# The DeltaNet's per-partition products as scaled copies on ScalarE, in a two-layer decoder trunk

## The chip, the cores and the metric

The kernel runs on one core of one Trainium2 chip. The metric is device time in microseconds for one launch of the whole trunk: 512 tokens of width 1024 through two layers. Weights and activations are fp32; TensorE's products are made of three passes on split operands (a high part `hi` rounded to fp32r, and the low part `x - hi`), so every weight that is loaded is first split by ScalarE (the high part) and VectorE (the low part).

## The reference

Each layer is a half-step SwiGLU, a mixer, a second half-step SwiGLU and a gated per-layer embedding, with an RMSNorm ahead of each. The mixer makes one input projection and parts its columns among an RG-LRU, sliding-window attention and a gated DeltaNet. Only the last is touched by the change. Per head (4 heads of width 64) and per chunk of 64 tokens it computes:

```python
gcum = jnp.cumsum(gc, axis=-1)
decay = jnp.exp(jnp.where(tril, gcum[..., :, None] - gcum[..., None, :], -jnp.inf))
k_beta = kc * bc[..., None]
v_beta = vc * bc[..., None]
Lmat = jnp.where(strict, jnp.einsum('...id,...jd->...ij', k_beta, kc) * decay, 0.0)
T = lax.linalg.triangular_solve(Lmat + eye, jnp.broadcast_to(eye, Lmat.shape), left_side=True,
                                lower=True, unit_diagonal=True)
u = jnp.einsum('...ij,...jd->...id', T, v_beta)
w = jnp.einsum('...ij,...jd->...id', T, k_beta * jnp.exp(gcum)[..., None])
```

and then a scan over chunks: `v_new = u - w @ state`, an output, and `state = state * exp(g_last) + k_dec^T @ v_new` with `k_dec = k * exp(g_last - g)`.

## The kernel before

Tokens lie on partitions in four tiles of 128 (`t` = 0 to 3); a tile holds two chunks of 64, and each tile carries the four heads side by side. The function `mixer` (called once per layer) issues, in this order: the projections that DeltaNet needs (`proj(0)` to `proj(5)`, and the product `ptm` in token layout), the small vectors (`beta`, `g`, norms), and then the DeltaNet stages below. Between them the call `fill(next(gaps, 0))` issues pieces of the rest of the mixer (the remaining projections `pp`, attention, RG-LRU), so that TensorE has work while the DeltaNet chain goes on; `GAPS` says how many microseconds of such pieces stand in each gap, and `ORDER` in which order they come.

TensorE's order is that of the program (`manual_schedule` for PE). The other engines' instructions are put in order by a scheduler that takes, from the instructions that are ready in its own timeline, the earliest in the program; those inside `tc.high_priority()` (the splits of `weight`, L119 on ScalarE and L120 on VectorE) come first. On the chip each engine then works through its queue strictly in that order.

The stages that the change touches:

- `masked(t)` (L1207 to L1213): for the high and the low part of `g`, the triangle `tri` (128x128) times one number per partition and head, into a tile `tg` of 128x512. One GpSimd instruction for each part. TensorE sums the two over partitions into `R` (L1220), the decay's exponent.
- `chunk(t)` (L1215 to L1257): `R`, the products `pk` of keys and queries with keys (L1227), the decay `DT` from `R` on ScalarE (L1231, L1233), its mask and scale on VectorE (L1236), the entries of `LTA` and `aT` (L1246, L1248), `er` and `qg`, and last `vk[t]`'s upper half (the keys times `eg`, L1252) and `kd[t]` (the keys times `cd`, L1255), each one GpSimd instruction of 128x256.
- the calls, in program order: `masked(0)`, `masked(1)`, a gap, the small products `pc` with `gc`, `eg`, `cd` and `egl`, and then for each `t`: `chunk(t)`, a gap, `masked(t + 2)`.
- `pv`: the values are transposed by TensorE, two tiles at a time, and VectorE scales them by `vr` into `vk[t]`'s lower half (L1289).
- Behind these, VectorE inverts the triangular blocks: transposes L1300, fifteen steps of substitution (L1310 to L1312), `TMA` (L1317), and TensorE joins the blocks in two levels (`pinv`, L1332, L1339, L1344), where ScalarE copies `pn` (L130). `vk` is first used by `products(0)` (L1381), `kd` by `steps(0)` (L1402).

The tiles `tg`, `DT`, `vk` and several others come from one pool of 14 slots (tag `d`). In the same stretch `fill` issues `lru_conv`: ScalarE's first tap (L875) and VectorE's three others (L877).

Of the kernel before, what the change touches and what calls it, by code (L numbers as in the profile page):

```python
# [9 lines left out]
F32 = mybir.dt.float32  # L10
# [4 lines left out]
AF = mybir.ActivationFunctionType  # L15
ALU = mybir.AluOpType
# [42 lines left out]
def trunk(ctx: ExitStack, tc: tile.TileContext, a):  # L59
    nc = tc.nc  # L60
    V, A, G, T = nc.vector, nc.scalar, nc.gpsimd, nc.tensor
# [7 lines left out]
    def bank(shape, name):  # L69
        return banks.tile(shape, F32, tag="b", name=name)  # L70
# [11 lines left out]
    tri = cst[:, K_TRI:K_TRI + 128]  # L82
# [742 lines left out]
    def mixer(l, norm, gain, ahead):  # L825
        xh, xl = norm.xh, norm.xl
        pl = par[:, l, :]
        with ExitStack() as es:
# [7 lines left out]
            def d2(shape, name):  # L836
                return dp.tile(shape, F32, tag="d", name=name)
# [17 lines left out]
            def small(name, n=16, **kw):  # L855
                return tp.tile([128, n], F32, tag=name, name=name, **kw)
# [209 lines left out]
            def fill(us):  # L1066
                while us > 0:
                    c = next(fill_, None)
                    if c is None:
                        return  # L1070
                    us -= c
# [28 lines left out]
            ktm = Pair([2, 128], "ktm")  # L1100
# [18 lines left out]
            for p in range(2):  # L1119
                pt = bank([128, 2, 2, 128], "ptk")  # L1120
                for i in range(2):
                    t = 2 * p + i
# [11 lines left out]
            def v3(x):  # L1134
# [7 lines left out]
                            in1=pl[:, C_DTB:C_DTB + 4].unsqueeze(1).to_broadcast([128, NT, 4]), op=ALU.add)  # L1142
# [5 lines left out]
            def hc(x):  # L1148
# [8 lines left out]
                                   in1=ea.unsqueeze(1).to_broadcast([128, NT, 4]),  # L1157
# [7 lines left out]
            vr = small("vr")  # L1165
# [36 lines left out]
            vk = [d2([128, 4, 128], "vk") for t in range(NT)]  # L1202
            aT = [None] * NT
            kd = Pair([2, 128], "kd")
# [3 lines left out]
            def masked(t):  # L1208
                tg[t] = [dp.tile([128, 4, 128], F32R, tag="d", name="tg") for x in range(2)]
                for o, x in zip(tg[t], (gh, gl_)):  # L1210
                    G.tensor_tensor(out=o, in0=tri.unsqueeze(1).to_broadcast([128, 4, 128]),
                                    in1=x.bitcast(F32)[:, 4 * t:4 * t + 4].unsqueeze(2).to_broadcast([128, 4, 128]),
                                    op=ALU.mult)  # L1213

            def chunk(t):  # L1215
                tsl = slice(t * 128, (t + 1) * 128)

                R = bank([128, 4, 128], name="R")
                for i, x in enumerate(tg[t]):
                    T.matmul(out=R.rearrange("p h i -> p (h i)"), lhsT=ones_r, rhs=x.rearrange("p h i -> p (h i)"),  # L1220
                             start=i == 0, stop=i == 1)

                pks = [bank([128, 2, 2, 128], "pk") for hh in range(2)]
                for c in range(2):
                    for hh in range(2):
                        r0 = 64 * hh
                        T.matmul(out=pks[hh][:, c], lhsT=kq[r0:r0 + 64, c, 0, tsl], rhs=kq[r0:r0 + 64, c, :, tsl],  # L1227
                                 start=True, stop=True)
                DT = d2([128, 4, 128], "DT")
                for h in range(4):  # L1230
                    A.activation(out=DT[:, h, :], in_=R[:, h, :], func=AF.Relu, scale=-1.0,  # L1231
                                 bias=gc[:, 4 * t + h:4 * t + h + 1])
                A.activation(out=DT, in_=DT, func=AF.Exp, scale=-1.0)  # L1233

                for h in range(4):
                    V.scalar_tensor_tensor(out=DT[:, h, :], in0=DT[:, h, :], scalar=b2[:, 4 * t + h:4 * t + h + 1],  # L1236
                                           in1=tri, op0=ALU.mult, op1=ALU.mult)
                er = small("er", 256)
                for hh in range(2):
                    rs = slice(64 * hh, 64 * hh + 64)  # L1240
                    A.activation(out=er[rs].rearrange("p (c i) -> p c i", c=2), in_=R[rs, 2 * hh:2 * hh + 2, :],
                                 func=AF.Exp)
                G.tensor_tensor(out=qg[t], in0=kq[:, :, 1, tsl], in1=er.rearrange("p (c i) -> p c i", c=2),
                                op=ALU.mult)
                for hh, pk in enumerate(pks):
                    V.tensor_tensor(out=LT[t][:, 2 * hh:2 * hh + 2, :], in0=pk[:, :, 0, :],  # L1246
                                    in1=DT[:, 2 * hh:2 * hh + 2, :], op=ALU.mult)
                    V.tensor_tensor(out=DT[:, 2 * hh:2 * hh + 2, :], in0=pk[:, :, 1, :],  # L1248
                                    in1=DT[:, 2 * hh:2 * hh + 2, :], op=ALU.mult)
                aT[t] = DT  # L1250
                kv = ktm[t].rearrange("p c (h d) -> p h c d", h=2)
                G.tensor_tensor(out=vk[t][:, :, 64:128].rearrange("p (h c) d -> p h c d", h=2), in0=kv,  # L1252
                                in1=eg[:, 4 * t:4 * t + 4].rearrange("p (h c) -> p h c", h=2).unsqueeze(3)
                                .to_broadcast([128, 2, 2, 64]), op=ALU.mult)
                G.tensor_tensor(out=kd[t].rearrange("p c (h d) -> p h c d", h=2), in0=kv,  # L1255
                                in1=cd[:, 4 * t:4 * t + 4].rearrange("p (h c) -> p h c", h=2).unsqueeze(3)
                                .to_broadcast([128, 2, 2, 64]), op=ALU.mult)  # L1257

            fill(next(gaps, 0))
            masked(0)  # L1260
            masked(1)
            fill(next(gaps, 0))
            pc = bank([128, 4, 16], "pc")
# [4 lines left out]
            eg = small("eg")  # L1268
            A.activation(out=eg, in_=pc[:, 0, :], func=AF.Exp)
            cd = small("cd")  # L1270
# [5 lines left out]
            for t in range(NT):  # L1276
                chunk(t)
                fill(next(gaps, 0))
                if t + 2 < NT:
                    masked(t + 2)  # L1280
            for p in range(2):
                pv = bank([128, 2, 2, 128], "pv")
                for i in range(4):
                    t = 2 * p + i // 2
                    T.transpose(out=pv[:, i // 2, i % 2, :], in_=s2[i % 2][:, t * 128:(t + 1) * 128], identity=ident)
                for i in range(2):
                    t = 2 * p + i

                    V.tensor_tensor(out=vk[t][:, :, 0:64].rearrange("p (h c) e -> p h c e", h=2),  # L1289
                                    in0=pv[:, i].rearrange("p c (h e) -> p h c e", h=2),  # L1290
                                    in1=vr[:, 4 * t:4 * t + 4].rearrange("p (h c) -> p h c", h=2).unsqueeze(3)
                                    .to_broadcast([128, 2, 2, 64]), op=ALU.mult)
                fill(next(gaps, 0))


# [2 lines left out]
            for q in range(4):  # L1298
                rs = slice(32 * q, 32 * q + 32)
                V.transpose(out=l32[rs].rearrange("p u j -> p (u j)"),  # L1300
                            in_=LTA[rs].rearrange("p t h i -> p (t h) i")[:, :, 32 * q:32 * q + 32])
# [11 lines left out]
            for t in range(NT):  # L1313
                if t == 0:
# [3 lines left out]
                                in0=x16[:, 4 * t:4 * t + 4, :].unsqueeze(2).to_broadcast([128, 4, 8, 16]),  # L1318
                                in1=cst[:, K_B16:K_B16 + 8].unsqueeze(1).unsqueeze(3).to_broadcast([128, 4, 8, 16]),
                                op=ALU.mult)  # L1320
# [170 lines left out]
            o = PAIRED  # L1491
# [7 lines left out]
            for c in range(2):  # L1499
                py = bank([128, S], "py")  # L1500
                for t in range(NT):
                    T.transpose(out=py[:, t * 128:(t + 1) * 128],
                                in_=oo[t // 2][:, t % 2, 2 * c:2 * c + 2, :].rearrange("p h e -> p (h e)"), identity=ident)
# [122 lines left out]
    for l in range(L):  # L1626
        pl = par[:, l, :]
        norm = rest(f, norm, pl[:, C_MX:C_MX + 8])
        f = ffn(l, 2)
        norm = mixer(l, norm, pl[:, C_F2:C_F2 + 8], f)  # L1630
        norm = rest(f, norm, pl[:, C_PL:C_PL + 8])
        f = ffn(l + 1, 1) if l + 1 < L else None
        norm = ple(l, norm, par[:, l + 1, C_F1:C_F1 + 8] if f else None, f)
# [123 lines left out]
```

## Time and profile before

| what | value |
| --- | --- |
| median of 3 runs (lowest to highest) | 2029.34 us (2026.89 to 2031.62) |
| the profiled execution's own time | 2028.79 us |
| its span | 2027.0 us |
| TensorE busy | 1975.1 us (97% of the span) |
| VectorE busy | 1485.6 us (73%) |
| ScalarE busy | 988.1 us (49%) |
| GpSimd busy | 142.7 us (7%) |
| chain that ended last: TensorE | 86% of the span |

TensorE is PE in the rows, ScalarE ACT, VectorE DVE, GpSimd POOL. A timeline row has the start and the duration in us from the span's start, the engine, the line, the operation, the tiles (out<-in), the shape and the count; where several were merged, the duration covers all of them. Square brackets hold the idle time of the engine just before and what ended it. Neighbouring instructions of one engine overlap a little, so starts are the safer measure of pace. PEclk is TensorE's granted clock as a share of full speed.

### The profile page before, as it was taken

Reading aid. Unit: us, or ns where it says so; the run is one execution under the profiler, and the core shown is the slowest. Engines: PE = TensorE matmul, PEld = TensorE weight load, DVE = VectorE, ACT = ScalarE, POOL = GpSimd, SP = SyncE. Lnnn points to the kernel's source line nnn. Section 1 sums busy time; section 2 is a strip of 40 time slices with the busy share of each in tenths; the row PEclk is TensorE's granted clock in tenths of the full one; section 3 lists DMA queues with packets and bytes.
Section 4 is the critical chain, followed back from the end, with each engine's and each line's share of the span. In section 5 each row is a group of like instructions: output and inputs, shape, how many; then the busy total and the mean of one; then the engine's idle time right before and its main releaser. Section 6 shows DMA issues by size and latency. Waiting matters only on the chain.

```text
span 2027.0 us, 32034 instructions
## 1 busy us (share of the span) xinstructions
PE 1975.1 (97%) x12657; PEld 1757.5 (87%) x12657; DVE 1485.6 (73%) x2603; ACT 988.1 (49%) x1633; POOL 142.7 (7%) x170
## 2 busy tenths in 40 slices
PE   8999999998999999999999999999899999999997
PEld 7988998886779989998889799988676899899886
DVE  6875873889868856865788568657887787488466
ACT  5643552455745534543555346434375555255343
POOL 0000000041200000000000000000311000000000
PEclk8999999998999999999999999999999999999998
DMA  6753743221053735745337357423112367275421
GB/s 212 190 168 100 187 119 121 79 73 55 9 166 101 203 112 147 179 124 135 120 101 201 105 150 176 124 80 104 53 34 68 105 172 183 78 193 138 134 66 63
DMA packets 83687, 249.79 MB, mean 123 GB/s; under 512 B 9424, under 2 KB 16848, under 8 KB 83280
## 3 DMA queue, kind: packets, MB, share of 16 engines
q1 hardware_dynamic: 72016, 205.79, 31.8%
q0 software_dynamic: 11520, 41.95, 11.8%
q8 instruction: 99, 1.62, 0.3%
q14 instruction: 52, 0.43, 0.1%
HBM read 245.61 MB, written 2.10 MB: 122 GB/s over the span
## 4 chain that ended last, share of the span: by engine, by line
PE 86%; DVE 6%; ACT 4%; DMA 2%; issue 1%; SPq 0%; DVEq 0%; ACTq 0%
PE pu L466 10%; PE pg L466 10%; PE pd L143 8%; PE pd L145 8%; PE pd L144 8%; PE qg L466 8%; PE qu L466 8%; PE pp L143 2%; PE pp L145 2%; PE pp L144 2%; PE pg L617 2%; PE pu L617 2%; PE ppg L143 1%; PE ppg L145 1%; PE ppg L144 1%
## 5 line engine op out<-in xcount | busy, mean ns | idle before, releaser
L466 PE MATMUL pg<-T,gh 128*128 128x256 f32 x832 | 150.4, 279 | 0.0
L119 ACT ACTIVATE wh<-wr 128x1024 fp32r<-128x1024 f32 (+2 forms) x76 | 77.1, 1014 | 144.9 <-PE pp L144 54.5
L434 DVE TENSOR_TENSOR gl<-wr,gh 128x1024 fp32r<-128x1024 f32 x96 | 117.5, 1224 | 35.5 <-ACT gh L429 35.5
L125 DVE TENSOR_TENSOR gl<-wr,gh 128x1024 fp32r<-128x1024 f32 x56 | 68.6, 1224 | 99.4 <-ACT gh L124 99.1
L466 PE MATMUL pu<-T,gh 128*128 128x256 f32 x736 | 133.6, 280 | 0.0
L120 DVE TENSOR_TENSOR wl<-wr,wh 128x1024 fp32r<-128x1024 f32 (+2 forms) x76 | 89.5, 1178 | 59.7 <-ACT wh L119 59.1
L124 ACT ACTIVATE gh<-wr 128x1024 fp32r<-128x1024 f32 x56 | 59.3, 1058 | 142.7 <-PE pd L144 63.6
L466 PEld LDWEIGHTS pg<-T,gh 128*128 128x128 f32 x832 | 127.3, 188 | 0.3
L429 ACT ACTIVATE sh<-r 128x512 fp32r<-128x512 f32 x80 | 50.6, 633 | 139.7 <-DVE r L446 139.7
L466 PE MATMUL pg<-T,gl 128*128 128x256 f32 x416 | 116.1, 279 | 0.0
L466 PEld LDWEIGHTS pu<-T,gh 128*128 128x128 f32 x736 | 112.6, 188 | 0.0
L429 ACT ACTIVATE gh<-wr 128x1024 fp32r<-128x1024 f32 x96 | 100.6, 1048 | 23.6 <-PE pd L144 23.6
L145 PE MATMUL pp<-X,wl 128*128 128x512 f32 x240 | 97.8, 408 | 7.3 <-DVE wl L120 7.3
L466 PE MATMUL pu<-T,gl 128*128 128x256 f32 x368 | 102.8, 279 | 0.0
L143 PE MATMUL pd<-X,gh 128*128 128x512 f32 x256 | 101.1, 395 | 0.0
L143 PE MATMUL pd<-X,wh 128*128 128x512 f32 x256 | 101.1, 395 | 0.0
L143 PE MATMUL pp<-X,wh 128*128 128x512 f32 x240 | 100.9, 420 | 0.0
L145 PE MATMUL pd<-X,gl 128*128 128x512 f32 x256 | 100.5, 393 | 0.0
L145 PE MATMUL pd<-X,wl 128*128 128x512 f32 x256 | 100.5, 393 | 0.0
L144 PE MATMUL pd<-X,gh 128*128 128x512 f32 x256 | 99.9, 390 | 0.0
L144 PE MATMUL pd<-X,wh 128*128 128x512 f32 x256 | 99.9, 390 | 0.0
L434 DVE TENSOR_TENSOR gl<-r,gh 128x1024 fp32r<-128x1024 f32 x52 | 63.6, 1224 | 48.9 <-ACT gh L429 48.8
(447 smaller groups left out, 6103.9 us busy)
## 6 DMA issues: line engine op xcount, KB each, us to landing
wr<-in_d_dram SPq DMA_DIRECT2D x64, 512.0 KB, 3.7
wr<-in_g_dram SPq DMA_DIRECT2D x48, 512.0 KB, 4.4
wr<-in_u_dram SPq DMA_DIRECT2D x48, 512.0 KB, 3.9
r<-in_g_dram SPq DMA_DIRECT2D x40, 512.0 KB, 3.9
r<-in_u_dram SPq DMA_DIRECT2D x40, 512.0 KB, 4.1
r<-in_g_dram POOLq DMA_DIRECT2D x40, 512.0 KB, 7.0
r<-in_u_dram POOLq DMA_DIRECT2D x40, 512.0 KB, 6.8
wr<-in_wi_dram SPq DMA_DIRECT2D x30, 512.0 KB, 3.3
```

What stands on the lines that cost most here:

```text
L119: A.activation(out=hi, in_=raw, func=AF.Copy)
L120: V.tensor_tensor(out=lo, in0=raw, in1=hi.bitcast(F32), op=ALU.subtract)
L124: A.activation(out=hi, in_=x, func=AF.Copy)
L125: V.tensor_tensor(out=lo, in0=x, in1=hi.bitcast(F32), op=ALU.subtract)
L143: T.matmul(out=out, lhsT=wh, rhs=xh, start=start, stop=False)
L144: T.matmul(out=out, lhsT=wh, rhs=xl, start=False, stop=False)
L145: T.matmul(out=out, lhsT=wl, rhs=xh, start=False, stop=stop)
L429: A.activation(out=self.g[n][0], in_=self.of(n)[0], func=AF.Copy)
L434: V.tensor_tensor(out=g[1], in0=raw, in1=g[0].bitcast(F32), op=ALU.subtract)
L466: T.matmul(out=ps, lhsT=l_[:, q, :], rhs=r_, start=start and q == 0 and i == 0, stop=stop and q == 3 and i == 2, skip_group_check=more)
L617: T.matmul(out=o[:, cs], lhsT=w_[:, b, :], rhs=x_, start=q + j + n + cs.start == 0, stop=q == 3 and j == 1 and n == 2, skip_group_check=True)
```

## The change

Every product with one number per partition is written as one ScalarE copy per head, with that number as the copy's scale. `masked` becomes eight copies of 128x128 per tile `t`, `vk`'s upper half and `kd` four copies of 128x64 each per tile, and `vk`'s lower half four copies of 128x64 per tile that read PSUM. The GpSimd instructions of L1211, L1252 and L1255 and the VectorE instruction of L1289 are gone. Shapes, tiles, the order of TensorE and the gaps stay as they were.

```diff
             def masked(t):
                 tg[t] = [dp.tile([128, 4, 128], F32R, tag="d", name="tg") for x in range(2)]
                 for o, x in zip(tg[t], (gh, gl_)):
-                    G.tensor_tensor(out=o, in0=tri.unsqueeze(1).to_broadcast([128, 4, 128]),
-                                    in1=x.bitcast(F32)[:, 4 * t:4 * t + 4].unsqueeze(2).to_broadcast([128, 4, 128]),
-                                    op=ALU.mult)
+                    for h in range(4):
+                        A.activation(out=o[:, h, :], in_=tri, func=AF.Copy, scale=x.bitcast(F32)[:, 4 * t + h:4 * t + h + 1])
...
-                kv = ktm[t].rearrange("p c (h d) -> p h c d", h=2)
-                G.tensor_tensor(out=vk[t][:, :, 64:128].rearrange("p (h c) d -> p h c d", h=2), in0=kv,
-                                in1=eg[:, 4 * t:4 * t + 4].rearrange("p (h c) -> p h c", h=2).unsqueeze(3)
-                                .to_broadcast([128, 2, 2, 64]), op=ALU.mult)
-                G.tensor_tensor(out=kd[t].rearrange("p c (h d) -> p h c d", h=2), in0=kv,
-                                in1=cd[:, 4 * t:4 * t + 4].rearrange("p (h c) -> p h c", h=2).unsqueeze(3)
-                                .to_broadcast([128, 2, 2, 64]), op=ALU.mult)
+                for h in range(4):
+                    kv = ktm[t][:, h % 2, 64 * (h // 2):64 * (h // 2) + 64]
+                    A.activation(out=vk[t][:, h, 64:128], in_=kv, func=AF.Copy, scale=eg[:, 4 * t + h:4 * t + h + 1])
+                    A.activation(out=kd[t][:, h % 2, 64 * (h // 2):64 * (h // 2) + 64], in_=kv, func=AF.Copy,
+                                 scale=cd[:, 4 * t + h:4 * t + h + 1])
...
-                    V.tensor_tensor(out=vk[t][:, :, 0:64].rearrange("p (h c) e -> p h c e", h=2),
-                                    in0=pv[:, i].rearrange("p c (h e) -> p h c e", h=2),
-                                    in1=vr[:, 4 * t:4 * t + 4].rearrange("p (h c) -> p h c", h=2).unsqueeze(3)
-                                    .to_broadcast([128, 2, 2, 64]), op=ALU.mult)
+                    for h in range(4):
+                        A.activation(out=vk[t][:, h, 0:64], in_=pv[:, i, h % 2, 64 * (h // 2):64 * (h // 2) + 64],
+                                     func=AF.Copy, scale=vr[:, 4 * t + h:4 * t + h + 1])
```

## Rows read from the trace of the kernel before

**Rows 1.** The page, busy us, share of the span, instructions

```profile
PE 1975.1 (97%) x12657; PEld 1757.5 (87%) x12657; DVE 1485.6 (73%) x2603; ACT 988.1 (49%) x1633; POOL 142.7 (7%) x170
```

**Rows 2.** Waits of TensorE, whole span: us in total, times, longest

```profile
PE pp L145 <- DVE wl L120: 7.3, 2, 3.7
PE pinv L1339 <- ACT pn L130: 4.0, 2, 2.0
...
PE pk L1227 <- DVE xs L868: 0.8, 1, 0.8
```

**Rows 3.** Windows behind a wait: busy by engine, clock, DMA share, GB/s

```profile
460.30:470.00 9.70, 8.90 (x30) 6.67 (x30) 7.96 (x22) 1.06 (x1) 0.00 (x0) 0.71 0.30 109
493.00:500.00 7.00, 6.88 (x34) 6.38 (x35) 7.00 (x12) 3.91 (x7) 0.00 (x0) 0.76 0.21 52
...
1455.10:1465.00 9.90, 7.99 (x30) 5.94 (x30) 9.10 (x26) 1.06 (x1) 0.00 (x0) 0.83 0.35 108
```

**Rows 4.** Window of the DeltaNet chunks: PE, PEld, DVE, ACT, POOL busy

```profile
428.00:457.00 29.00, 27.81 (x134) 20.55 (x132) 25.69 (x48) 15.62 (x38) 17.54 (x20) 1.00 0.12 37
```

**Rows 5.** Timeline of VectorE

```profile
434.61 0.75 DVE L877 SCALAR_TENSOR_TENSOR T<-xs,par,T 128x512 f32<-128x512 f32 x1
...
441.78 3.34 DVE L1236 SCALAR_TENSOR_TENSOR DT<-DT,b,cst 128x128 f32<-128x128 f32 x4
...
453.91 1.13 DVE L1236 SCALAR_TENSOR_TENSOR DT<-DT,b,cst 128x128 f32<-128x128 f32 x4
...
459.04 1.23 DVE L120 TENSOR_TENSOR wl<-wr,wh 128x1024 fp32r<-128x1024 f32 x1
...
461.03 0.76 DVE L1289 TENSOR_TENSOR vk<-pv,vr 128x256 f32<-128x256 f32 x2
...
483.38 3.79 DVE L1317 TENSOR_TENSOR TMA<-x,cst 128x512 f32<-128x512 f32 x4
...
1478.32 3.34 DVE L1317 TENSOR_TENSOR TMA<-x,cst 128x512 f32<-128x512 f32 x4
```

**Rows 6.** Timeline of GpSimd, first product of each layer

```profile
428.22 1.04 POOL L1211 TENSOR_TENSOR tg<-cst,gh 128x512 fp32r<-128x512 f32 x1 [3.43 <-ACT gh L124]
...
1422.35 1.04 POOL L1211 TENSOR_TENSOR tg<-cst,gh 128x512 fp32r<-128x512 f32 x1 [3.21 <-ACT gh L124]
```

**Rows 7.** Timeline of ScalarE

```profile
429.60 1.06 ACT L119 ACTIVATE wh<-wr 128x1024 fp32r<-128x1024 f32 x1 [1.46 <-PE pp L144]
...
434.69 0.18 ACT L1269 ACTIVATE eg<-pc 128x16 f32<-128x16 f32 x1 [3.32 <-DVE gc L1267]
...
446.08 0.81 ACT L875 ACTIVATE T<-xs,par 128x512 f32<-128x512 f32 x1 [5.15 <-DVE xs L868]
446.92 1.14 ACT L1231 ACTIVATE DT<-R,gc 128x128 f32<-128x128 f32 x4
447.94 0.77 ACT L1241 ACTIVATE er<-R 64x256 f32<-64x256 f32 x2
...
449.39 1.15 ACT L1231 ACTIVATE DT<-R,gc 128x128 f32<-128x128 f32 x4
...
451.73 1.05 ACT L119 ACTIVATE wh<-wr 128x1024 fp32r<-128x1024 f32 x1
...
476.47 0.69 ACT L130 ACTIVATE e<-e,dn 128x128 f32<-128x128 f32 x2 [0.81 <-DVE dn L972]
```

**Rows 8.** Timeline of TensorE: sums of the fourth chunk, first inverse product

```profile
444.58 0.73 PE L1220 MATMUL R<-tg,ones_r 128*128 128x512 f32 x2
446.10 1.85 PE L1227 MATMUL pk<-kq 64*128 64x256 f32 x8 [0.80 <-DVE xs L868]
...
485.69 1.95 PE L1332 MATMUL pinv<-TMA,LTA 128*128 128x128 f32 x16
...
1440.52 0.73 PE L1220 MATMUL R<-tg,ones_r 128*128 128x512 f32 x2
1481.18 1.95 PE L1332 MATMUL pinv<-TMA,LTA 128*128 128x128 f32 x16
```

## The prediction

> **What bounds the kernel now.** I read the busy times first, then TensorE's waits, then its granted clock in windows behind the longest, and then the four queues by time in the DeltaNet stage. TensorE is busy for 1975 of 2027 us, ScalarE for 988 [rows 1]. So the end is set by TensorE's row of matmuls, which is written out by hand, and a change pays only by the waits of that row and by the clock that a wait costs. Few waits lie where the change works, and the larger come once per layer [rows 2]: 3.7 us for the low part of a weight (VectorE, L120), 2.0 us for the negated product of the inverse (ScalarE, L130), and, in the first layer alone, 0.8 us ahead of `pk`. The reader is to see in the windows behind the first two what a wait costs besides itself [rows 3]: granted 0.71 over 9.7 us and 0.83 over 9.9 us behind the 3.65 us waits, 0.76 over 7 us behind a 2 us wait. That is 9.7 x 0.29 = 2.8 us, 1.7 us and 1.7 us of full-speed work not granted.
>
> The changed instructions stand from `masked(0)` (428.2 us) to the second `pv`. Between 428 and 457 us VectorE is busy 25.7 of 29 us, ScalarE 15.6, GpSimd 17.5 [rows 4]. VectorE is the crowded engine there, and part of its crowding comes from GpSimd: four L1236 instructions take 3.34 us while GpSimd multiplies and 1.13 us once it has stopped [rows 5]. That is why L120 of the weight for which TensorE waits 3.65 us, until 460.3, starts only at 459.04, although ScalarE's half, started at 451.73, was done by 452.8 [rows 5, 7].
>
> **The change, part by part.** A GpSimd product of `masked` takes 1.04 us [rows 6]; 16 of these and 16 of 128x256 go, with 8 of VectorE's (0.76 us for two [rows 5]). ScalarE gets 160 copies with a scale per partition, 80 a layer.
>
> Price of a copy. Nearest row for the 32 of 128x128: two ScalarE copies from SBUF with such a scale take 0.69 us together. Neighbours overlap by some 0.1 us (four L1231 last 1.14, but the next instruction starts 1.02 after their first), so each lasts 0.39 and the pace is 0.30 [rows 7]. For the 48 of 128x64 no row stands: above 0.18 us, what a 128x16 takes, and below 0.30. I take 0.245, halfway, for the 32 that read SBUF. For the 16 that read PSUM I take 0.21, since four 128x128 from PSUM come in 1.02 us, 0.255 each [rows 7]. Sum per layer: 32 x 0.30 + 32 x 0.245 + 16 x 0.21 = 9.6 + 7.8 + 3.4 = 20.8 us; with the bounds 18.2 to 25.4 us (0.345, half of the pair, and 0.30). The Trainium skill (ScalarE: Activation LUTs, What ACT_TABLE_LOAD costs) gives 186 ns plus 0.833 ns an element plus 93 ns for a scale read per partition, with 93 ns overlapped between neighbours, an estimate of 0.239 us for 64 columns and a sum of 20.9; no row here shows that width.
>
> Against it ScalarE has 29 - 15.6 = 13.4 us free in the first 29 us. So the copies fit the layer, but not the moment: this is the step on which the rest hangs.
>
> When ScalarE's queue gets to `masked(3)`. All engines but TensorE are ordered by the scheduler, from what is ready by place in the program. In that order ScalarE does before the last copy of `masked(3)`: 32 copies of `masked` (9.6), 16 copies of `vk` and `kd` for two chunks (3.9), the decays of two chunks at 2.47 us each (446.92 to 449.39), two weight conversions at 0.97, and 0.4 of small ones [rows 7]: 9.6 + 3.9 + 4.9 + 1.9 + 0.4 = 20.8 us. Counted from 428.2 that is 449.0. TensorE wants it at 444.58 in the first layer [rows 8]: 4.4 us late. In the second layer it wants it at 1440.52, with GpSimd's first product at 1422.35: 2.6 us late. `masked(2)` comes out at about 442, just ahead of its matmul.
>
> Cost of that wait. First layer: 4.4 late, 2.8 for the clock as behind the 3.65 us wait, less the 0.8 that `pk` waits now for VectorE [rows 8], which goes because VectorE is early there: +6.4 us. Second layer: 2.6 + 1.7 = +4.3. That wait is on the path, since TensorE has nothing else in its row.
>
> What goes. VectorE loses four vk products a layer and its neighbour on SBUF: 2.2 us for a chunk whose L1236 overlapped with GpSimd. It then stands waiting for ScalarE's decays, so L120 has nothing ahead of it. Its weight is ready at about 459, and TensorE, 6.4 us later than before, asks at 463. The two waits and their clock go: -3.65 - 2.8 = -6.45 and -3.65 - 1.7 = -5.35. If that cover fails, both stay.
>
> What is late next. VectorE's way to the inverse. The last decay is out of ScalarE near 456.5 (449.0 + 2.47 + 2.0 of copies + 2.4 + 0.97), VectorE's part of the chunk (1.13 for L1236 and 1.5 for four products of L1289's size) near 459.1, against 453.91 + 2.6 = 456.5 now: 2.6 later. The two convolutions (six L877), which VectorE did in gaps, now come behind, since their first step (L875) gives way on ScalarE: six at 0.75 less the overlap of neighbours, 4.4 us. Less 1.5 for L1289, and less the 1.7 us that VectorE is idle between 460.3 and 470 [rows 3], the first `TMA` is 3.8 us later: 484.3 (483.38 and a quarter of 3.79) becomes 488.1. TensorE now starts `pinv` at 485.69 [rows 5, 8], so 2.4 late, plus 1.7 clock. The wait for L130 (2.0) and its clock (1.7), a little behind, are swallowed: +0.4. In the second layer it is out at 1479.2 + 3.8 = 1483.0 against 1481.18: 1.8 + 1.7 - 3.7 = -0.2.
>
> These last two replace what was saved before, since TensorE waits there for VectorE whatever it had in hand: the layers end at about +0.4 and -0.2. ScalarE's queue runs in order, and now a conversion that waits for TensorE holds copies behind it; today it has waited 1.46 us so and 5.15 us behind a convolution [rows 7]. Bounds 0 and 5.15; I take 1.0 a layer, nearer the first, as the second came from VectorE's crowding. Sum: +0.4 - 0.2 + 2.0 = +2.2 us on the profiled execution's 2028.79 (span 2027.0 and 1.8 around it), 2031.0; the median of the runs shown, 2029.34, stands 0.55 above that execution, so 2031.5.
>
> **The rivals.**
> Relief decides, faster. ScalarE puts `masked(3)` ahead of the `vk` and `kd` copies (3.9 us), which nothing needs before `products(0)`. Then the matmul is at most 0.5 us late, no clock is lost, and VectorE's relief counts in full: -0.8 + 0.5 - 6.45 and -5.35, about -12 us, 2017. For it: GpSimd's products, too, were taken as they became ready. Against it: program order puts the copies first. The Trainium skill (SBUF — State Buffer, Who interferes with whom) says that a VectorE instruction with two SBUF inputs and a GpSimd one that reads SBUF share a read interface, and the one that comes second blocks in full; by that rule the relief is complete, which would favour this rival. The trace agrees, with 3.34 against 1.13 us.
>
> ScalarE becomes the bound, slower. A weight conversion (L119) stands behind copies, so its low part is late again where L120 is late now. This decides from some 4 us of extra queue, which the upper price (25.4 against 20.8) or one wait at the head of 5 us brings. The two waits with their clock then stay: +11.8 on my sum, 2043. For it: 20.8 us put on 13.4 free. Against it: conversions have high priority.
>
> All is hidden: the copies fall into idle time, VectorE's relief into its own, 2029.
>
> **How the numbers follow.** No change of note, as summed: 0.42, its own range 2026 to 2037. Relief decides: 0.24. ScalarE the bound: 0.26. All hidden: 0.08. A measurement of this kernel tells some 0.2%, 4 us, from no change: 2025.3 to 2033.4. Faster by more: 0.22 of the second and 0.03 of the first, 0.25; within: 0.28 of the first, 0.07 of the last, 0.35; slower: 0.40. The range for all goes from the whole relief and a little, 2016, to the bound with 5 us of waits at the head of its queue, 2048.
>
> **What would show it.** Right: TensorE idle ahead of `R` of the fourth chunk by 3 to 5 us (first layer) with ScalarE as releaser; no wait for L120 near 456; L1236 near 1.13 us per four in all chunks; ScalarE's copies at 0.30 and 0.245 apart. Wrong: no wait at `R`, or the L120 wait still there; `TMA` earlier than 484; or a difference that lies outside the two DeltaNet stages.

## The result, and the profile after

The changed kernel takes 2063.26 us (median of 4 runs, 2056.65 to 2064.6), against 2028.12 for the kernel before beside it (4 runs, 2026.43 to 2031.62): 1.0165 times as long, 95% interval 1.0138 to 1.0191. That is 35 us slower, and above the stated range (2016 to 2048). The profiled execution took 2063.24 us, its span 2061.2.

First the page of after, then the waits of TensorE over the whole span (us in total, times, longest). They answer to [rows 1, 2].

```profile
PE 1981.2 (96%) x12657; PEld 1763.5 (86%) x12657; DVE 1472.0 (71%) x2595; ACT 1026.5 (50%) x1791; POOL 116.5 (6%) x138
```

```profile
PE pinv L1328 <- DVE TMA L1313: 30.2, 2, 15.1
...
PE R L1219 <- ACT tg L1212: 7.5, 4, 2.7
...
PE pp L145 <- DVE wl L120: 0.4, 1, 0.4
```

ScalarE has 38 us more, VectorE 14 and GpSimd 26 less, as planned. One line of waits is new and large: TensorE waits 15.1 us in each layer for `TMA`, the input of the inverse. The wait at `R` is new too. The one for the low weight (7.3 us) is down to 0.4, and the one for `pn` (4.0) is gone.

How much of the difference lies in the DeltaNet stages? The windows below reach in each layer from the first `pc` to the first `pwo`. Columns: us, busy us of PE, PEld, DVE, ACT and POOL, then the granted clock, DMA share and GB/s. Before:

```profile
432.40:561.90 129.50, 120.39 (x753) 91.16 (x751) 113.68 (x342) 79.06 (x198) 29.73 (x35) 0.96 0.11 37
1428.30:1557.40 129.10, 120.87 (x754) 91.31 (x752) 111.47 (x342) 79.08 (x198) 28.62 (x34) 0.96 0.12 37
```

The same windows after:

```profile
437.90:582.00 144.10, 121.83 (x754) 92.45 (x752) 107.31 (x339) 94.37 (x262) 20.17 (x22) 0.92 0.10 33
1447.30:1593.20 145.90, 123.00 (x753) 92.98 (x752) 107.37 (x339) 94.27 (x262) 20.19 (x22) 0.89 0.10 33
```

These two stretches grow from 258.6 to 290.0 us, by 31.4 of the span's 34.2. TensorE's busy time in them grows by 3.6 only (244.8 against 241.3), which is matmuls at a lower granted clock (0.92 and 0.89 against 0.96); its idle time grows by 27.8.

All of it lies ahead of the inverse: from the first `pc` to the first `pinv` after takes 68.8 and 71.5 us in the two layers, where before took 53.3 and 52.9; behind that it is 0.9 and 1.8 us shorter than before.

Where does the 15 us wait come from? VectorE's timeline of after, first layer (start, us, engine and line, operation; in brackets the idle time before it and its releaser):

```profile
445.16 1.14 DVE L1235 SCALAR_TENSOR_TENSOR DT<-DT,b,cst 128x128 f32<-128x128 f32 x4 [2.03 <-ACT DT L1232]
...
459.75 1.14 DVE L1235 SCALAR_TENSOR_TENSOR DT<-DT,b,cst 128x128 f32<-128x128 f32 x4 [3.94 <-ACT DT L1232]
...
475.96 0.42 DVE L1306 STREAM_SHUFFLE row<-er 128x240 f32<-128x240 f32 x1
...
487.58 0.69 DVE L914 SCALAR_TENSOR_TENSOR T<-sq,T 128x512 f32<-128x512 f32 x1 [1.20 <-ACT sq L912]
...
492.19 0.69 DVE L914 SCALAR_TENSOR_TENSOR T<-sq,T 128x512 f32<-128x512 f32 x1 [2.77 <-ACT sq L912]
...
495.69 0.69 DVE L925 SCALAR_TENSOR_TENSOR tm<-tm,T 128x512 f32<-128x512 f32 x1 [1.40 <-ACT sq L918]
...
498.38 0.69 DVE L925 SCALAR_TENSOR_TENSOR tm<-tm,T 128x512 f32<-128x512 f32 x1 [1.06 <-ACT T L924]
...
504.49 1.23 DVE L930 TENSOR_TENSOR_SCAN T<-tm,T 128x512 f32<-128x512 f32 x1
...
505.63 2.06 DVE L1313 TENSOR_TENSOR TMA<-x,cst 128x512 f32<-128x512 f32 x2
```

The same instructions before:

```profile
464.10 0.42 DVE L1310 STREAM_SHUFFLE row<-er 128x240 f32<-128x240 f32 x1
...
481.80 0.69 DVE L914 SCALAR_TENSOR_TENSOR T<-sq,T 128x512 f32<-128x512 f32 x1 [0.39 <-ACT sq L912]
...
487.10 0.68 DVE L914 SCALAR_TENSOR_TENSOR T<-sq,T 128x512 f32<-128x512 f32 x1
...
492.62 1.29 DVE L925 SCALAR_TENSOR_TENSOR tm<-tm,T 128x512 f32<-128x512 f32 x2 [2.44 <-ACT sq L918]
```

The reader is to see two chains in one queue. The first shuffle to `TMA` is the forward substitution, which builds the small triangular inverses (L1306 to L1313). Lines 914 to 930 belong to the RG-LRU, a branch that TensorE does not need yet. Before, one of its products stood ahead of `TMA` (481.80; `TMA` at 483.38 [rows 5]), and all others behind. After, all twelve instructions stand ahead, both scans included, in both layers. VectorE takes its queue in order, so the substitution also stands still while an RG-LRU product waits for ScalarE: 1.20 + 2.77 + 1.40 + 1.06 = 6.4 us of idle time inside the inversion. The substitution takes 29.7 us (475.96 to 505.63), where it took 19.3; it also starts later, 38.1 us behind the first `pc` against 31.7.

ScalarE meanwhile, in after:

```profile
432.09 1.28 ACT L1212 ACTIVATE tg<-cst,gh 128x128 fp32r<-128x128 f32 x4
433.28 1.26 ACT L1212 ACTIVATE tg<-cst,gl__4265 128x128 fp32r<-128x128 f32 x4
...
458.00 0.81 ACT L1253 ACTIVATE T<-T,cd 128x64 f32<-128x64 f32 x3
458.83 0.37 ACT L1230 ACTIVATE DT<-R,gc 128x128 f32<-128x128 f32 x1
459.10 0.62 ACT L1232 ACTIVATE DT<-DT 128x512 f32<-128x512 f32 x1
...
463.31 0.62 ACT L1232 ACTIVATE DT<-DT 128x512 f32<-128x512 f32 x1
...
466.37 1.75 ACT L1287 ACTIVATE vk<-pv,vr 128x64 f32<-128x64 f32 x8 [1.49 <-PE pv L1282]
...
489.60 1.28 ACT L911 ACT_TABLE_LOAD   x1
```

The decays (L1232), for which VectorE waits 3.94 us at 459.75, stand behind ten key copies, of which the row at 458.00 holds the last three. A load of another function table between the RG-LRU's functions takes 1.28 us here, and one of them lies in the 2.77 us that VectorE stands still. The Trainium skill (ScalarE: Activation LUTs, What ACT_TABLE_LOAD costs) gives 1283 ns for the load, and the trace agrees with that part. The page adds some 1380 ns for a drain; no row here shows one, since the instruction before this load ends at 489.58 and the next starts at 490.89, so here the measurement decides.

TensorE's own row in after, with the three places where it waits longest:

```profile
452.84 0.49 PE L1219 MATMUL R<-tg,ones_r 128*128 128x512 f32 x1 [2.69 <-ACT tg L1212]
454.53 0.65 PE L1219 MATMUL R<-tg,ones_r 128*128 128x512 f32 x1 [1.19 <-ACT tg L1212]
...
506.73 3.78 PE L1328 MATMUL pinv<-TMA,LTA 128*128 128x128 f32 x16 [15.10 <-DVE TMA L1313]
```

The first 16 `pinv` take 3.78 us behind that wait, against 1.95 before [rows 8]. The window of after over them shows why, with a granted clock of 0.50 (1.2 GHz) after 15 us of idle time; in before (first line) it is 1.00 over these matmuls.

```profile
485.60:487.60 2.00, 2.00 (x19) 1.96 (x18) 2.00 (x3) 1.98 (x5) 0.42 (x1) 1.00 0.00 0
...
506.70:510.20 3.50, 3.47 (x17) 3.47 (x17) 3.50 (x6) 0.60 (x1) 0.45 (x1) 0.50 0.00 0
```

### The profile page after: what moved, and what is told of

Its sections match the earlier page's. It is cut to its first block, busy times and chain, and to the rows that moved or that the text cites. A ratio compares the mean times of both kernels' runs of the same rounds, so it can differ in the third digit from the quotient of the medians.

```text
span 2061.2 us, 32139 instructions
## 1 busy us (share of the span) xinstructions
PE 1981.2 (96%) x12657; PEld 1763.5 (86%) x12657; DVE 1472.0 (71%) x2595; ACT 1026.5 (50%) x1791; POOL 116.5 (6%) x138
## 4 chain that ended last, share of the span: by engine, by line
PE 84%; ACT 7%; DVE 6%; DMA 1%; issue 1%; DVEq 0%; SPq 0%; ACTq 0%
PE pu L466 10%; PE pg L466 10%; PE pd L143 8%; PE pd L145 8%; PE pd L144 8%; PE qg L466 8%; PE qu L466 7%; PE pp L143 2%; PE pg L617 2%; PE pp L144 2%; PE pp L145 2%; PE pu L617 2%; PE ppg L143 1%; PE ppg L145 1%; PE pwo L145 1%; PE ppg L144 1%
## 5 line engine op out<-in xcount | busy, mean ns | idle before, releaser
L120 DVE TENSOR_TENSOR wl<-wr,wh 128x1024 fp32r<-128x1024 f32 (+2 forms) x76 | 88.9, 1170 | 70.1 <-ACT wh L119 69.6
L466 PE MATMUL pu<-T,wh 128*128 128x256 f32 x544 | 98.2, 279 | 0.0
```

Source lines behind the costliest of these rows:

```text
L120: V.tensor_tensor(out=lo, in0=raw, in1=hi.bitcast(F32), op=ALU.subtract)
L466: T.matmul(out=ps, lhsT=l_[:, q, :], rhs=r_, start=start and q == 0 and i == 0, stop=stop and q == 3 and i == 2, skip_group_check=more)
```

## The experiments

Two theories stood from the start. A: the loss is the order of VectorE's queue, that is, RG-LRU products ahead of the inversion. B: ScalarE's copies cost it by their own time, wherever the RG-LRU stands. The table gives the median, the ratio to the kernel before beside it with its 95% interval, the wait of `pinv` for `TMA` (total of both layers; "none" where no such wait shows), and by how much the two `pc`-to-`pwo` stretches of the profiled execution differ from the 258.6 us of before.

| run | us | ratio (interval) | `pinv` waits for `TMA` | two stages |
|---|---|---|---|---|
| the change | 2063.26 | 1.0165 (1.0138 to 1.0191) | 30.2 | +31.4 |
| e1 masked alone | 2031.76 | 1.002 (1.001 to 1.003) | 13.1 | -1.3 |
| e2 keys alone | 2054.51 | 1.0134 (1.0116 to 1.0151) | 30.9 | +27.1 |
| e3 values alone | 2027.73 | 1.0005 (0.9996 to 1.0015) | none | +0.8 |
| e4 the change, edges | 2040.38 | 1.0065 (1.0041 to 1.0089) | 0.2 | +8.8 |
| e5 before, edges | 2025.65 | 0.9994 (0.9985 to 1.0003) | none | -2.1 |
| e6 masked, edges | 2026.17 | 0.9993 (0.9984 to 1.0001) | 0.4 | -8.7 |
| e7 masked and values, edges | 2020.8 | 0.9961 (0.9948 to 0.9975) | none | -12.0 |
| e8 the change, keys late, edges | 2033.69 | 1.0035 (1.0022 to 1.0047) | none | +1.6 |
| e9 keys alone, edges | 2035.1 | 1.0034 (1.0022 to 1.0047) | 2.1 | +6.3 |
| e10 the change, keys late | 2042.25 | 1.0074 (1.0052 to 1.0096) | 8.7 | +13.9 |
| e11 masked and values | 2022.63 | 0.9973 (0.9956 to 0.9991) | 5.7 | -4.7 |

**e1, e2, e3: one part of the change each.** Masked alone keeps this hunk, with the others as before:

```diff
+                    for h in range(4):
+                        A.activation(out=o[:, h, :], in_=tri, func=AF.Copy, scale=x.bitcast(F32)[:, 4 * t + h:4 * t + h + 1])
```

> Only the masked decays go to ScalarE; keys, decayed keys and values stay on GpSimd and VectorE. Theory A (order): the loss comes from RG-LRU steps that stand ahead of VectorE's inversion in its queue; here only some of them do, so the first inverse product waits 5 to 10 us a layer for TMA, total 2038 to 2050. Theory B (lateness alone): the matmul R waits for the copies as in the changed kernel (about 3.9 us a layer) and that, passed on with its clock, is most of the loss: 2048 to 2060.

Keys alone keeps the copies of `vk` and `kd` with `eg` and `cd`:

```diff
+                    A.activation(out=vk[t][:, h, 64:128], in_=kv, func=AF.Copy, scale=eg[:, 4 * t + h:4 * t + h + 1])
+                    A.activation(out=kd[t][:, h % 2, 64 * (h // 2):64 * (h // 2) + 64], in_=kv, func=AF.Copy,
+                                 scale=cd[:, 4 * t + h:4 * t + h + 1])
```

> Only the upper half of vk and kd go to ScalarE. Theory A: here too all but a few RG-LRU steps stand ahead of the inversion, so the wait for TMA is 10 to 15 us a layer though R waits for nothing, total 2048 to 2062. Theory B: no copy stands ahead of R, the decays are late by at most 4 us, total 2028 to 2038.

Values alone keeps the copies out of `pv`:

```diff
+                        A.activation(out=vk[t][:, h, 0:64], in_=pv[:, i, h % 2, 64 * (h // 2):64 * (h // 2) + 64],
+                                     func=AF.Copy, scale=vr[:, 4 * t + h:4 * t + h + 1])
```

> Only the lower half of vk (values, from PSUM) goes to ScalarE; VectorE loses 1.5 us a layer. Both theories: no RG-LRU step ahead of the inversion, no wait at R, total within 4 us of before (2024 to 2032).

The 32 key copies a layer alone bring 27 of the 35 us, the others nearly nothing: 4 us for masked, less than either theory gave, and none for the values. In e1 `pinv` waits 6.6 us a layer for `TMA`, as A had it, and no `R` waits, against B; that it costs so little fits the waits for the low weight and for `pn` (7.3 and 4.0 us before), which are gone in e1. VectorE's timeline with the keys alone shows the order of after:

```profile
481.75 0.69 DVE L914 SCALAR_TENSOR_TENSOR T<-sq,T 128x512 f32<-128x512 f32 x1 [1.11 <-ACT sq L912]
...
497.97 1.22 DVE L930 TENSOR_TENSOR_SCAN T<-tm,T 128x512 f32<-128x512 f32 x1
...
500.05 2.16 DVE L1315 TENSOR_TENSOR TMA<-x,cst 128x512 f32<-128x512 f32 x2
```

**e4: the change, with the order held.** Edges without a semaphore (they bind the order in the queue, and the chip waits for nothing more) keep the four RG-LRU products (two L914, two L925) behind the last transpose of the inversion in VectorE's own queue; those that depend on them follow. Nothing is computed otherwise.

```diff
+                held.append(V.scalar_tensor_tensor(out=xr[i], in0=ti, scalar=1.0, in1=xr[i], op0=ALU.add, op1=ALU.mult))
...
+                last = V.transpose(out=ti.rearrange("p h i -> p (h i)"), in_=tm.rearrange("p h i -> p (h i)"))
...
+            for x in held:
+                tc.add_manual_dep(x.ins, last.ins.name,
+                                  mybir.DependencyInfo(mybir.DependencyClass.NoSync, mybir.DependencyReason.DATA), reason="inversion first")
```

> The changed kernel with four RG-LRU instructions of VectorE per layer queued behind the transposes of the inversion, so that no RG-LRU step stands ahead of it; nothing else differs. Theory A: the wait for TMA falls from 15.1 to about 5 us a layer, total 2038 to 2050. Theory B: TMA is late for ScalarE's sake, the wait stays above 12 us, total 2056 to 2065.

2040.4 us: of the 35 us some 23 come back by the medians, 20 by the ratios, with an edit that changes no work and no engine. VectorE's timeline, then TensorE's waits in that run (the line numbers are 2 higher here):

```profile
474.34 0.41 DVE L1308 STREAM_SHUFFLE row<-er 128x240 f32<-128x240 f32 x1
...
490.62 3.79 DVE L1315 TENSOR_TENSOR TMA<-x,cst 128x512 f32<-128x512 f32 x4
494.33 2.48 DVE L1320 STREAM_TRANSPOSE TT<-TMA 128x512 f32<-128x512 f32 x4
496.73 1.25 DVE L916 SCALAR_TENSOR_TENSOR T<-sq,T 128x512 f32<-128x512 f32 x2
```

```profile
PE R L1221 <- ACT tg L1214: 7.2, 4, 2.7
PE ptr L986 <- DVE e L136: 4.0, 2, 2.0
...
PE sc L955 <- DVE T L1047: 3.2, 2, 1.8
PE ptr L986 <- ACT e L130: 1.8, 4, 0.4
```

`TMA` now starts 54.3 us after the first `pc` (436.3), against 51.0 before and 67.7 in after; in the second layer 55.4, against 50.0 and 70.4. The substitution starts 38.0 us after `pc`, as in after (38.1): up to there the two are alike, and the order inside it makes the difference. What is left, 12.7 us, has its own waits: `R`, and the attention's `ptr` (5.8 in total, where before had 0.8) and `sc` (7.0 with the part that waits for `mx`, where before had 4.3).

**e5: do the edges do anything by themselves?**

> The kernel before, with its GpSimd and VectorE products, and with the four RG-LRU products (two L914, two L925) queued on VectorE behind the last transpose of the inversion. Theory A (what was lost is the order of VectorE's queue, and the kernel before had nearly that order already): 2024 to 2031 us, the waits for L120 (7.3 us) and for pn (4.0) as before. Theory B (the edges are worth time or cost time by themselves): below 2022 or above 2033; then the 23 us that they gave back in the changed kernel is not the undoing of a loss alone.

No: 0.9994, and the L120 wait (7.4 us) is still there. Only the wait for `pn` is not as A had it, 2.4 us in place of 4.0. So what e4 gave back was lost by the order, as A says.

**e6, e7, e11: without the keys.** e6 is e1 with the edges of e4; e7 adds the value copies of e3; e11 is e7 without the edges.

> The masked decays alone on ScalarE, and the four RG-LRU products behind the inversion in VectorE's queue. Theory A (the 6.6 us of waiting per layer that this part brought are the same reordering): the wait for TMA falls below 2 us per layer, and with the clock behind it some 8 us a layer come back less what the wait had swallowed: 2014 to 2023 us, faster than the kernel before by the relief of VectorE. Theory B (the inversion is late by the copies' own length): the wait stays at 4 us a layer or more, 2027 to 2033.

> The masked decays and the values on ScalarE, the keys on GpSimd as before, and the four RG-LRU products behind the inversion. Theory A: as with the masked decays alone, 2013 to 2023 us, since the values by themselves moved nothing (2027.7 against 2027.7). Theory B (value copies hold ScalarE's queue while they wait for TensorE, so that pn or a decay comes late): 2026 to 2034, with a wait on ScalarE ahead of pinv.

> The masked decays and the values on ScalarE, the keys on GpSimd, no edges. Theory A (the edges are what makes that kernel faster than before): 2028 to 2036 us, a wait for TMA of 4 to 8 us per layer as with masked alone. Theory B (values on ScalarE free VectorE enough that the order comes right by itself): 2016 to 2024, no such wait.

In e6 the wait for `TMA` went as A has it, but the time missed A's range: the profiled execution (2022.0) showed the stages 8.7 us shorter, the median of 11 runs is not told from before. e7 came out in its A's range and is faster than the kernel before, by 0.39% (0.25 to 0.52), and so is e11, by 0.27%. So for these two parts A fell in e11, which came out in B's 2016 to 2024, though not without a wait, as B had it (5.7 us are left): the edges are not what makes them faster, and between e7 and e11 the intervals overlap. What makes them faster is probably the relief that the change was to bring: the wait for the low weight (7.3 us before) is gone, and VectorE's four groups of L1237 take 5.5 us in e7's first layer, where L1236 took 8.9 before. That is argued and not shown, since e6 has both too. e7 has both stages at 0.99 of the clock in its profiled execution, which took 2014.4 us, 6.4 below the median of its five:

```profile
432.90:556.40 123.50, 117.27 (x753) 89.23 (x751) 108.07 (x339) 87.27 (x231) 24.76 (x30) 0.99 0.11 38
1422.40:1545.50 123.10, 117.36 (x754) 88.97 (x752) 106.70 (x338) 86.54 (x230) 24.22 (x30) 0.99 0.11 39
```

Its waits of TensorE hold neither `R` nor the low weight of `pp`:

```profile
PE pinv L1348 <- ACT pn L130: 4.2, 2, 2.1
PE pk L1228 <- ACT er L1242: 3.1, 2, 1.8
```

**e8, e10: the keys late.** The key copies of all chunks are issued behind the last chunk, with the edges (e8) and without (e10).

```diff
+            for t in range(NT):
+                for h in range(4):
+                    kv = ktm[t][:, h % 2, 64 * (h // 2):64 * (h // 2) + 64]
+                    A.activation(out=vk[t][:, h, 64:128], in_=kv, func=AF.Copy, scale=eg[:, 4 * t + h:4 * t + h + 1])
...
```

> The changed kernel with the four RG-LRU products behind the inversion, and with the key copies (vk, kd) of all four chunks issued behind the last chunk. Theory A (what is left above the kernel before, 12.7 us, is the wait at R and its clock, and the key copies stand in ScalarE's queue ahead of masked and of the decays): the wait at R (7.2 us in total) falls to 0 to 2, 2024 to 2033 us. Theory B (ScalarE has too much work in this stretch wherever the keys stand): the wait at R goes, but one for a decay, pn or a key takes its place: 2036 to 2044.

> The whole change, without edges, with the key copies of all four chunks issued behind the last chunk. Theory A (a few us of lateness of the last decay suffice for the scheduler to put RG-LRU products ahead of the inversion): a wait for TMA of 4 to 12 us per layer, 2038 to 2052 us. Theory B (only the place of the key copies made it): no such wait above 2 us, 2030 to 2036, as with edges (2033.7).

e10 came out in A's range, with A's wait in the first layer alone: `pinv` waits 8.7 us there, and in the second layer the order is right. The place of the keys gives back 21 us without edges (18 by the ratios). In e8 the wait at `R` went (0.7 us in total), and another took its place, as B has it:

```profile
PE pk L1228 <- DVE DT L1249: 6.2, 2, 3.4
```

`pk` waits for VectorE to read a bank, and VectorE for a decay that ScalarE does at 448.58:

```profile
444.80 1.28 ACT L1214 ACTIVATE tg<-cst,gh 128x128 fp32r<-128x128 f32 x4
...
447.16 1.04 ACT L119 ACTIVATE wh<-wr 128x1024 fp32r<-128x1024 f32 x1
448.11 0.57 ACT L1279 ACTIVATE T<-T,cd 128x64 f32<-128x64 f32 x2
448.58 0.61 ACT L1234 ACTIVATE DT<-DT 128x512 f32<-128x512 f32 x1
```

Ahead of it stand the masked copies of the last chunk, a weight conversion, and still two of the `kd` copies, which the later place in the program moved only in part. The time, 2033.7, lies between the two theories, nearer to A.

**e9: the keys alone, with the edges.**

> The key copies alone on ScalarE (masked and values as before), and the four RG-LRU products behind the inversion in VectorE's queue. Theory A (keys alone lose 27 us because the decays come late and the scheduler then puts the RG-LRU ahead of the inversion): the wait for TMA falls from 15.4 us to under 3 per layer, and 2027 to 2036 us. Theory B (ScalarE's key copies cost the time themselves): a wait of 8 us or more per layer stays ahead of pinv, 2044 to 2056.

```profile
PE pk L1229 <- ACT er L1243: 7.3, 2, 3.8
...
PE ptr L986 <- DVE e L136: 4.0, 2, 2.0
...
PE pinv L1336 <- DVE TMA L1317: 2.1, 2, 1.0
```

A: the wait for `TMA` falls from 30.9 to 2.1, and 2054.5 becomes 2035.1. So of the 27 us of the keys some 20 are the order. In the other 7, `pk` waits for a bank that ScalarE reads late (`er`), and `ptr` comes late as in e4. `ptr` waits for VectorE (L136) only in the runs that have both key copies and edges (e4, e8, e9), so whether that part is the keys' or the price of the edges is not shown.

## Why the prediction was wrong

**Priced rightly.** In after, four copies of 128x128 take 1.28 us and the next four start 1.19 us after them, 0.30 each as forecast. Of the 128x64 from SBUF three last 0.81 us and the next instruction starts 0.83 after the first; one by itself lasts 0.33, so the pace is (0.81 - 0.33) / 2 = 0.24, against 0.245. The eight from PSUM take 1.75 us, at most 0.22 each, against 0.21. The estimate by the Trainium skill's formula (ScalarE: Activation LUTs, What ACT_TABLE_LOAD costs), 0.239 us at 64 columns, agrees with the 0.24 from SBUF and is too high for PSUM. The order ahead of `masked(3)` was right too: in after, 16 key copies and two conversions stand ahead of its last copy, which ends 22.4 us after the first masked copy starts (20.8 forecast). The wait at `R` was put at 4.4 and 2.6 us; it is 2.69 + 1.19 = 3.9 in the first layer and the rest of 7.5, 3.6, in the second. The L120 wait went but for 0.4, and L1235 takes 1.14 us for four in all chunks, where four L1236 took up to 3.34 beside GpSimd [rows 5]. So the shared interface of the Trainium skill (SBUF — State Buffer, Who interferes with whom) agrees with the trace again.

**The step that failed** is "What is late next. VectorE's way to the inverse": "the first `TMA` is 3.8 us later". Counted from the first `pc`, it came 16.7 us later in the first layer and 20.4 in the second. What the step summed came out near: with the order of the queue held, e4's `TMA` is 3.3 and 5.4 us later. Luck had a part in that: the last decay came out 31.8 us after the first masked copy starts, where 28.3 was forecast, and only three of the six L877 came that late. What failed is that the step left VectorE's queue behind the decays in its old order, without naming that as a choice. That order is made by the scheduler before the run, and the changed program got another. The step moved the L877 products but did not ask where the RG-LRU products, the other work of that queue, would then stand. The 13.4 us between e4 and after are theirs: 6.4 of idle time in which VectorE waits for ScalarE, and 8.8 of their own length, from start to start (ten products and two scans), less 1.6 that VectorE waits less for TensorE inside the chain (0.39 against 1.98). The forecast 2.4 us at `pinv` became 15.1.

**A second step, behind the inverse.** With the order held the kernel is still 12.7 us slower than before, where +2.2 was forecast; 8.8 of that lies in the two stages of the profiled executions. Ahead of the first `pinv`, e4 is 2.2 and 3.8 us longer than before, near the 2.4 and 1.8 of the forecast. Behind it the sum had -2.0 a layer (1.7 for the clock, less 3.7 for the wait for L130 and its clock), and e4 is 0.7 and 2.1 us longer instead. The wait for L130 did go, but other waits took its place: `ptr`, a transposition for the attention that no term of the sum had, waits 5.0 us longer in both layers than before. The term of 1.0 a layer, for ScalarE's conversions that hold copies behind them, can't be told apart from these in any run.

**The rivals.** "ScalarE becomes the bound" had the sign but not the way: no conversion was late in after. "Relief decides" had as its condition that `masked(3)` comes ahead of the key copies. In e8 and e10 it does, but for some `kd` copies, and the wait at `R` goes as that rival says; but they take 2033.7 and 2042.3 us, where 2017 was forecast. What it lacked is that a decay then stands behind the masked copies and a weight conversion on ScalarE (`pk` waits 6.2 us in e8), and in e10 the order besides. Near its time comes e7, 2020.8, which has no key copies on ScalarE. "All is hidden" holds for the values alone (e3).

**What stays open.** By the rule in "The kernel before", the earliest in the program comes first among what is ready, and the program favours the RG-LRU: its gates and scan are issued in the 9.0 us gap ahead of the inversion. TensorE's row shows it, since 21 `pp` products, seven steps of three, stand between the gates' last product and `pinv`, while the 3.5 us gap behind the inversion issues only six steps (0.64 us each), so the gap ahead of it had gone past the scan. What held the RG-LRU back in the kernel before can then, by that rule, only be what the scheduler takes for ready, and its timeline is in no trace. Lateness on the chip alone does not settle it: in e1 the substitution starts 30.4 us after `pc`, against 31.7 before, and still both L914 and one L925 stand ahead of `TMA`:

```profile
482.73 0.69 DVE L914 SCALAR_TENSOR_TENSOR T<-sq,T 128x512 f32<-128x512 f32 x1 [2.79 <-ACT sq L912]
486.23 0.69 DVE L925 SCALAR_TENSOR_TENSOR tm<-tm,T 128x512 f32<-128x512 f32 x1 [1.52 <-ACT sq L918]
487.56 3.33 DVE L1316 TENSOR_TENSOR TMA<-x,cst 128x512 f32<-128x512 f32 x4
```

It is open too why masked and values together are faster than before, though neither is alone, and no run splits the keys' other 7 us between `vk` and `kd`.

## What to carry to other kernels

Where a scheduler orders the queues, a change of engine or length is also a change of order in every queue that shares the work: list what else stands in the critical engine's queue near the chain, and price each such instruction, with the wait at its head, as if it came first. A chain that must not wait can be held by edges within one queue, at no cost that a run can tell in the kernel before, whose order was nearly right already (0.9994); what is held back may then be late for others, as `ptr` may show. Of an offload in several parts, time the parts alone and together: here masked alone costs 0.2% and the values alone nothing, both together gain 0.27 to 0.39%, and the keys alone cost 1.3%.

## What the hardware showed besides

The 32 value copies cost nothing that a run can tell and the 64 key copies 27 us, at 0.2 to 0.3 us each: some 20 of these 27 us were not the engine's time but the order of the queues. A TensorE that waited 15.1 us did its next 16 matmuls in 3.78 us, against 1.95 us without such a wait, so a long wait is paid once more behind it.
